# An encoder trunk of saved products: a pair of eight forms that takes 7 or 8 products by block, 12 pages instead of 13, a smaller DMA scratch and new orders

## The chip, the cores and the metric

One core of one Trainium2 chip runs the whole kernel. The metric is the device time of one execution in microseconds (us), the median of three runs. TensorE is called PE here, with its weight loads apart as PEld; VectorE is DVE, ScalarE ACT, GpSimd POOL and SyncE SP.

## What is computed

Two layers of an encoder over 256 tokens and 4096 features, in float32. Each layer normalises its input, multiplies it with one input projection of 11264 columns, runs 16 attention heads (4 of them keys and values) and 8 bidirectional retention heads on the result, gates both and multiplies their 4096 columns with an output projection, which is added to the input. A last normalisation follows.

```python
for l in range(DEPTH):                       # 2
    proj = rmsnorm(x, norm_w[l]) @ w_in[l]   # 256 x 4096 by 4096 x 11264
    aq, ak, av, ag, rq, rk, rv, rg = jnp.split(proj, SPLIT_POINTS, axis=-1)
    a_out = silu(ag) * gqa_attention(rope(rms(aq)), rope(rms(ak)), av)
    r_out = silu(rg) * rmsnorm(bidirectional_retention(rope(rq), rope(rk), rv))
    x = x + jnp.concatenate([a_out, r_out], -1) @ w_out[l]   # 256 x 4096 by 4096 x 4096
return rmsnorm(x, final_norm)
```

Nearly all of the arithmetic is in the two projections.

## The kernel before

**Blocks and pairs.** The projections are cut into 30 blocks that PE works through one after the other. A block is 256 tokens by 1024 columns (two tiles of 512, for instance keys and values). Layer 0 has input blocks 0 to 10 and output blocks 11 to 14, layer 1 has 15 to 25 and 26 to 29; these four runs are the stages 0 to 3 of the code, and `(2, 7)` in a table is the block b = 7 of stage 2, which is block 22 here. A block sums over 4096 features, cut into 16 pairs of 2 x 128 features (`NP`). For each pair the operand and the weights are 2 x 2 tiles, and the block's results collect in the eight PSUM banks M1 to M8.

**Products.** A pair takes eight products of a 128 x 128 operand tile and a 128 x 512 weight tile, or seven, by a scheme of the Strassen kind, from sums of operand tiles and sums of weight tiles. A product is three matmuls, since each float32 factor is split into a high and a low part: high by high, low by high (both at line 1760), high by low (line 1770). The six pairs 2, 5, 8, 9, 11 and 13 (`SEVENS`) take seven in every block. Pairs 3 and 6 (`FLEX`) take eight, except in the last stage: there pair 3 takes seven in blocks 27 to 29 and pair 6 in blocks 27 and 28. That makes 185 pair-blocks of seven.

**Weights.** A pair of eight has two weight pages (A and B) of 128 x 1024 in each block. SP loads each (`wraw`), ACT casts it to its high part `whi`, DVE subtracts that to get the low part `wlo`. A pair of seven has A, a sum T, a sum U and a half page B: ACT copies A to `wv`, POOL adds the weights of `twice_in` or `twice_out` to it with an accumulating DMA (line 762), DVE makes `wu` from A, `wv` and a half page `third`, and all four are cast and subtracted like the others. Five high pages (`RING`) and four low ones (`LOWS`) can stand ahead of PE.

**Operands.** At the turn from stage to stage `split_pair` (line 822) makes the operand's parts: `x8h` and `x8l`, four tiles each, for pairs of eight, `x7h` and `x7l`, seven forms each, for pairs of seven, by way of a page `xf`. For the pairs in `FLEX` a task `more_forms` (line 894) fetches the stage's input again (`again`) and makes the four further forms in two pages, `xf` and `xs`.

**Pages and tasks.** Everything else in SBUF comes from 13 pages of 4 KB a partition (`PAGES`, `page`). Attention, retention, turns and block results are tasks that run beside the products; a task starts when as many pages are free as it needs (`NEED`, and `need=` where it is added), and blocks always keep two for their own results. `attention_values` (line 1352) splits the fetched page `pT` into two new pages. Each wait that PE would have is estimated while the program is built: `Clock` and `Now` keep planned times of the engines, and constants such as `STRICT`, `LOW_AHEAD` or `RELIEF`, set for each block from `PLANS` by `assume`, say how far ahead work is put. The emitted order on each engine is fixed by this.

**Order within a block.** The first block of a stage takes its pairs in `opening_order`, with the sevens at the places given by `SPREAD` to `SPREAD3`. The others take them in the plain order of their numbers, stage 3's later blocks by `LATE_SPREAD` and `END_SPREAD`.

Of the kernel before, what the change touches and what calls it, by code (L numbers as in the profile page):

```python
# [12 lines left out]
F32R = mybir.dt.float32r  # L13
# [4 lines left out]
P = 128  # L18
# [11 lines left out]
KG = 4  # L30
# [5 lines left out]
PAGES = 13  # L36
# [46 lines left out]
NEED = {"ak": 5, "ag": 3, "rk": 4, "rg": 4}  # L83
# [28 lines left out]
    1: {'LOW_AHEAD': 5.0},  # L112
    6: {'TIGHT_A': 8},
    7: {'SUM_SLACK': 0.0, 'AT_ONCE': 1, 'STRICT': 4},
    8: {'TIGHT_B': 5, 'STRICT': 5},
    9: {'THIRD_SLACK': 1.0, 'BANK_REST': 1.5, 'LOW_AHEAD': 1.0, 'RAW_SLACK': 1.0, 'RELIEF': 0.7, 'PASS': 0.1},
    14: {'STRICT': 9, 'TIGHT_A': 0},
    15: {'S_FIXED': 0.16, 'LONG': 2, 'EARLY': 1.8, 'PASS': 0.3, 'PE_REST': 2.0, 'NEAR': 30},
    22: {'PASS': 0.3, 'U_SLACK': 1.0, 'AT_ONCE': 1},
    24: {'V_FIXED': 0.12, 'TIGHT_B': 20, 'TIGHT_A': 2},  # L120
# [9 lines left out]
SEVENS = ((2, 5, 8, 9, 11, 13), (2, 5, 8, 9, 11, 13), (2, 5, 8, 9, 11, 13), (2, 5, 8, 9, 11, 13))  # L130

FLEX = (3, 6,)

LATER = [tuple(sorted(_s + (FLEX if _i == 3 else ()))) for _i, _s in enumerate(SEVENS)]

EVER = sorted(set(_p for _s in SEVENS for _p in _s))
TWICE = sorted(EVER + list(FLEX))
EIGHTS = [_p for _p in range(NP) if _p not in EVER]
# [16 lines left out]
BLOCKS = [(("ak", 0), ("av", 0))]  # L155
BLOCKS += [(("ag", _g), ("aq", _g)) for _g in range(4)]
for _r in range(2):
    BLOCKS += [(("rk", _r), ("rq", _r))]
    BLOCKS += [(("rg", 2 * _r + _i), ("rv", 2 * _r + _i)) for _i in range(2)]
# [8 lines left out]
def constants():  # L168
# [50 lines left out]
GROUPS = [  # L219
    ([tuple(range(_s[0]))] if _s[0] else []) + [tuple(range(_a, _b)) for _a, _b in zip(_s, _s[1:] + (NP,))] for _s in LATER  # L220
]
SPREAD = (3, 5, 8, 11, 12, 13)
SPREAD1 = (4, 7, 8, 10, 12, 14)
SPREAD2 = (2, 3, 6, 7, 10, 13)
SPREAD3 = (6, 7, 9, 11, 12, 14)


def opening_order(stage):

    spread = (SPREAD, SPREAD1, SPREAD2, SPREAD3)[stage]  # L230
    spread = spread if len(spread) == len(SEVENS[stage]) else SEVENS[stage]
    order = [_p for _p in ([1, 0] if stage == 0 else [0, 1]) + list(range(2, NP)) if _p not in SEVENS[stage]]
    for i, p in zip(spread, SEVENS[stage]):
        order.insert(i, p)
    return order
# [12 lines left out]
END_FLEX = (3,)  # L248
END_SPREAD = (1, 3, 5, 7, 9, 11, 12)
LATE_SPREAD = (1, 3, 5, 6, 8, 9, 11, 12)  # L250


def late_order(sevens, spread):

    order = [_p for _p in range(NP) if _p not in sevens]
    for i, p in zip(spread or sevens, sevens):
        order.insert(i, p)
    return order


GROUPS[3] = grouped(late_order(LATER[3], LATE_SPREAD), LATER[3])
END_SEVENS = tuple(sorted(SEVENS[3] + END_FLEX))
END_GROUPS = grouped(late_order(END_SEVENS, END_SPREAD or LATE_SPREAD), END_SEVENS)


def plan_of(stage, b):

    if not b:
        return FIRST_GROUPS[stage], SEVENS[stage]
    if stage == 3 and b == N_OUT2 - 1:  # L270
        return END_GROUPS, END_SEVENS
    return GROUPS[stage], LATER[stage]
# [3 lines left out]
FIRST_GROUPS = [grouped(_o, SEVENS[_i]) for _i, _o in enumerate(FIRST_ORDER)]  # L276
LEADS = [8 * next(_i for _i, _p in enumerate(_o) if _p in SEVENS[_s]) for _s, _o in enumerate(FIRST_ORDER)]
# [91 lines left out]
def hybrid_encoder(  # L369
# [38 lines left out]
    def f32(v):  # L408
        return v.bitcast(F32)
# [412 lines left out]
    def split_pair(p, v, whole, stage):  # L822
# [15 lines left out]
        if p in SEVENS[stage]:  # L838
# [12 lines left out]
            ve.tensor_sub(s1, a22, x1[:, 0])  # L851
            ve.scalar_tensor_tensor(s2, s1, -1.0, x0[:, 0], op0=ALU.mult, op1=ALU.subtract)
            ve.tensor_sub(s3, x0[:, 0], x1[:, 0])
            ve.tensor_add(s4, x0[:, 1], s2)
            yield
            ac.copy(hi[:, 2:7, :], f)
            ve.tensor_sub(tokens(lo[:, 0:2, :]), x0, tokens(f32(hi)[:, 0:2, :]))
            yield
            ve.tensor_sub(lo[:, 2:7, :], f, f32(hi)[:, 2:7, :])
            sums_of.pop()  # L860
            drop()
        else:
            if p in EIGHTS:
                hi = t(ap, [P, 2, SEQ], "x8h", len(EIGHTS), F32R)
                lo = t(ap, [P, 2, SEQ], "x8l", len(EIGHTS), F32R)
            else:
                both = [t(ap, [P, 7, P], v, len(EVER), F32R) for v in ("x7h", "x7l")]
                hi, lo = (v[:, 0:4, :].rearrange("p (i m) t -> p i (m t)", m=MT) for v in both)
            if whole is None:
                u = [w.rearrange("p i (m a t) -> p i m a t", m=MT, t=BLK) for w in (hi, lo)]  # L870
                pieces = [(u[0][:, i], u[1][:, i], v[:, :, i]) for i in range(2)]
            else:
                pieces = [(hi, lo, whole)]
            for h, _, src in pieces:
                ac.copy(h, src)
            yield
            for h, w, src in pieces:
                ve.tensor_sub(w, src, f32(h))
        version[p] += 1
        if version[p ^ 1] == version[p]:  # L880
            drop()
        if stage == 3 and p in FLEX:
            tasks.append(Lane(more_forms(p), need=3, gate=forms_due))
# [468 lines left out]
    def attention_values(g, h, kv, sgT):  # L1352
# [4 lines left out]
        parts = parts_of("pT", [P, KG * SEQ])  # L1357
        yield from split(parts, pT)
        drop()
# [149 lines left out]
    def retention_pair(L, i, gacc, vacc):  # L1509
# [4 lines left out]
        v = yield from values(vacc, L)  # L1514
        yield
# [90 lines left out]
    def lead(stage):  # L1606

        return 8 * (late_order(LATER[3], LATE_SPREAD).index(LATER[3][0]) if stage == 3 else SEVENS[stage][0])

    def block(after_pair, phase, then, first_order=False, opening=False, order=LAST_ORDER, last=None, hurried=False):  # L1610
# [9 lines left out]
        groups, sevens = plan_of(stage, 0 if opening else N_OUT2 - 1 if last else 1)  # L1620
# [6 lines left out]
        if 0 not in SEVENS[stage] or first_order:  # L1627
# [27 lines left out]
        def begin_product(n, name, p, index, k, h):  # L1655
# [27 lines left out]
            elif p in sevens and p in FLEX:  # L1683
# [15 lines left out]
        after = 0 if not then else lead(then - 1) if then == phase else LEADS[then - 1]  # L1699

        def end_product(n, name, p, index, k, h):
# [360 lines left out]
    for l, L in enumerate(layers):  # L2062
        for bi, (one, _) in enumerate(BLOCKS):
# [10 lines left out]
            c = block(after, 2 * l + 1, 2 * l + 1 + (bi == N_IN - 1), start, bi == 0)  # L2074
# [11 lines left out]
        for n in range(N_OUT2):  # L2086
# [12 lines left out]
            if last_layer and final:  # L2099
# [4 lines left out]
                block(after, 2 * l + 2, 0, order=FINAL_ORDER, last=last_combine(res))  # L2104
                follow(True)
            else:
                if final:
                    turning.append(Turn(2 * l + 2))
                c = block(after, 2 * l + 2, 2 * l + 2 + (n == N_OUT2 - 1), opening=n == 0, hurried=n == 0)
                tasks.append(Lane(out_tasks(l, n, c), need=4, own=2))  # L2110
# [62 lines left out]
```

## Time and profile before

| | us |
|---|---|
| median of three runs | 2594.49 |
| lowest, highest | 2593.19, 2596.14 |
| the profiled execution's span | 2591.4 |
| PE busy in it | 2577.2 |
| DVE busy | 2233.3 |
| ACT busy | 1864.9 |
| POOL busy | 403.7 |

The span is from the first to the last instruction of one execution. What lies around it in a run's time, 3.1 us against the median, has no instructions. Busy times are sums over the engine's own instructions; matmuls overlap in them, so that a matmul is listed with 389 ns although the next one starts earlier.

### The profile page before, as it was taken

What the parts mean: (1) busy time and instruction counts of PE and PEld (TensorE: products, weight loads), DVE (VectorE), ACT (ScalarE), POOL (GpSimd) and SP (SyncE); (2) the same over time, 40 slices, a digit from 0 to 9 for tenths busy, and PEclk for the clock granted to TensorE, in tenths of its full rate; (3) what the DMA queues carried; (4) which work ended last, traced back from release to release, by engine and by line L of the source; (5) the groups of instructions that cost most, each with busy time, mean ns of one, the idle gap of its engine ahead of it and who ended that gap; (6) DMA issues with size and microseconds to landing.
All of it is one profiled execution on the core that took longest, in us unless ns stands there. A gap on an engine that the chain in (4) does not pass through costs nothing.

```text
span 2591.4 us, 34411 instructions
## 1 busy us (share of the span) xinstructions
PE 2577.2 (99%) x11545; PEld 2132.6 (82%) x11545; DVE 2233.3 (86%) x2740; ACT 1864.9 (72%) x2643; POOL 403.7 (16%) x555
## 2 busy tenths in 40 slices
PE   9999999999999999999999999999999999999998
PEld 7888888888888888888878888888888888888886
DVE  7898888889789898877988888889888798989887
ACT  8877776766576788655987667777666667887665
POOL 0112221221102101211111112221201021011100
PEclk9999999999999999999999999999999999999999
DMA  9988988888778777988888889888887797789986
GB/s 317 301 243 275 285 243 254 282 251 256 224 227 255 233 228 224 276 267 245 284 251 260 251 242 280 243 270 262 260 261 223 207 270 234 221 245 259 256 263 196
DMA packets 207601, 655.88 MB, mean 253 GB/s; under 512 B 24896, under 2 KB 31552, under 8 KB 207424
## 3 DMA queue, kind: packets, MB, share of 16 engines
q1 hardware_dynamic: 147040, 471.68, 51.9%
q0 software_dynamic: 59664, 180.91, 31.5%
q8 instruction: 90, 1.47, 0.2%
q10 hardware_dynamic: 720, 1.10, 0.1%
q14 instruction: 87, 0.71, 0.1%
HBM read 609.55 MB, written 44.04 MB: 252 GB/s over the span
## 4 chain that ended last, share of the span: by engine, by line
PE 97%; DVE 1%; DMA 1%; ACT 1%; issue 0%; SPq 0%; POOLq 0%; POOL 0%; DVEq 0%; ACTq 0%
PE M L1760 62%; PE M L1770 31%; PE M L1225 1%; PE M L1224 1%; PE M L1223 1%; DMA ca<-in_x 0%; PE M L1754 0%; DVE cb L353 0%; DVE wlo L353 0%; ACT ca L353 0%; DVE ca L353 0%; DMA whole<-in_w_in 0%; ACT whi L353 0%; ACT wv L353 0%; DVE x7h L353 0%
## 5 line engine op out<-in xcount | busy, mean ns | idle before, releaser
L353 DVE TENSOR_TENSOR wlo<-wraw,whi 128x1024 fp32r<-128x1024 f32 (+1 forms) x769 | 929.8, 1215 | 159.3 <-PE M L1770 52.8
L353 ACT CAST whi<-wraw 128x1024 fp32r<-128x1024 f32 (+1 forms) x771 | 795.8, 1045 | 279.1 <-PE M L1760 263.2
L1760 PE MATMUL M<-whi,x8h 128*128 128x512 f32 x2338 | 910.8, 390 | 0.5 <-DVE ca L353 0.3
L1760 PE MATMUL M<-whi,x8l 128*128 128x512 f32 x2338 | 910.0, 389 | 0.0
L1770 PE MATMUL M<-wlo,x8h 128*128 128x512 f32 x2334 | 669.4, 389 | 0.0
L1760 PEld LDWEIGHTS M<-whi,x8h 128*128 128x128 f32 x2338 | 439.0, 188 | 93.1 <-DVE ca L353 1.0
L1760 PEld LDWEIGHTS M<-whi,x8l 128*128 128x128 f32 x2338 | 439.0, 188 | 91.0 <-issue 0.2
L1770 PEld LDWEIGHTS M<-wlo,x8h 128*128 128x128 f32 x2334 | 436.5, 188 | 89.9 <-DVE wlo L353 0.7
L1760 PE MATMUL M<-whi,x7h 128*128 128x512 f32 x1080 | 420.5, 389 | 0.2 <-ACT whi L353 0.2
L1760 PE MATMUL M<-whi,x7l 128*128 128x512 f32 x1080 | 420.3, 389 | 0.0
L1770 PE MATMUL M<-wlo,x7h 128*128 128x512 f32 x1080 | 334.2, 389 | 0.2
L762 POOL DMA_DIRECT2D wv<-in_twice_in x132 | 118.5, 897 | 1068.4 <-ACT wv L353 909.3
L353 ACT CAST whi<-wu 128x1024 fp32r<-128x1024 f32 x185 | 194.6, 1052 | 98.2 <-DVE wu L353 61.5
L353 ACT CAST whi<-wv 128x1024 fp32r<-128x1024 f32 x185 | 194.2, 1050 | 87.5 <-PE M L1760 50.7
L353 DVE TENSOR_TENSOR wlo<-wv,whi 128x1024 fp32r<-128x1024 f32 x185 | 225.7, 1220 | 34.1 <-PE M L1770 26.9
L353 ACT COPY wv<-wraw 128x1024 f32<-128x1024 f32 x185 | 194.2, 1050 | 74.5 <-DMA wraw<-in_w_out 32.2
L353 DVE TENSOR_TENSOR wlo<-wu,whi 128x1024 fp32r<-128x1024 f32 x185 | 225.3, 1218 | 20.6 <-PE M L1770 13.7
L1770 PEld LDWEIGHTS M<-wlo,x7h 128*128 128x128 f32 x1080 | 202.6, 188 | 42.9 <-DVE wlo L353 1.0
L1760 PEld LDWEIGHTS M<-whi,x7h 128*128 128x128 f32 x1080 | 202.8, 188 | 42.4 <-ACT whi L353 0.8
L1760 PEld LDWEIGHTS M<-whi,x7l 128*128 128x128 f32 x1080 | 202.8, 188 | 41.7
L353 DVE TENSOR_TENSOR wu<-wraw,wv 128x512 f32<-128x512 f32 x185 | 126.6, 685 | 10.6 <-DMA wv<-in_twice_in 8.4
L353 DVE TENSOR_TENSOR wu<-wu,third 128x512 f32<-128x512 f32 x185 | 128.0, 692 | 6.4
(261 smaller groups left out, 2346.3 us busy)
## 6 DMA issues: line engine op xcount, KB each, us to landing
wraw<-in_w_in SPq DMA_DIRECT2D x568, 512.0 KB, 5.2
wraw<-in_w_out SPq DMA_DIRECT2D x203, 512.0 KB, 5.4
wv<-in_twice_in POOLq DMA_DIRECT2D x132, 512.0 KB, 7.7
third<-in_w_in SPq DMA_DIRECT2D x132, 256.0 KB, 5.7
wv<-in_twice_out POOLq DMA_DIRECT2D x53, 512.0 KB, 8.1
third<-in_w_out SPq DMA_DIRECT2D x53, 256.0 KB, 5.8
full<-next_dram POOLq DMA_DIRECT2D x18, 512.0 KB, 9.3
p_dram<-room POOLq DMA_DIRECT2D x64, 128.0 KB, 3.5
```

What stands on the lines that cost most here:

```text
L353: return call(out, *args, **kwargs)
L762: self.adds.pop(0)[1]()
L1223: nc.tensor.matmul(out, a[0], b[0], start=start, stop=False)
L1224: nc.tensor.matmul(out, a[0], b[1], start=False, stop=False)
L1225: nc.tensor.matmul(out, a[1], b[0], start=False, stop=stop)
L1760: nc.tensor.matmul(acc[name], a[i], g.hi[h], start=m == first[name] and not i, stop=False)
L1770: nc.tensor.matmul(acc[name], a, g.lo[h], start=False, stop=m == final[name])
```

## The change

Pair 6 leaves `FLEX` and the pairs of eight and becomes a pair of a new kind (`RESIDENT`): its operand holds eight forms, the four plain tiles and the four sums, made once at each of the four turns, in new tiles `xfh` and `xfl`. So each block can take seven or eight products of it; the table `ACTIVE` gives it seven in the blocks (0, 7), (2, 2), (2, 7), (3, 1) and (3, 2), which are blocks 7, 17, 22, 27 and 28. Pair 3 stays as it was, in a table by block.

Space for it: `PAGES` goes from 13 to 12, the scratch of the software DMAs from 4096 to 1024 bytes, and pair 6 gives its two tiles of eight back. `attention_values` writes the low part of `pT` into the page of `pT` itself. The pages that tasks must find free to start fall by one for the key block, for `attention_rest` and for the output blocks, and two tasks lower their claim to 3 once they have split their values.

Orders: the openings of stages 1, 2 and 3 get new places for the sevens (stage 0 keeps its own), the later blocks of stage 1 and blocks of seven sevens get new ones (`LATES`); the later blocks with six sevens in stages 0 and 2 keep the plain order. Which product leads the next block is now read from the block itself. `PLANS` is rewritten for 19 of the 30 blocks.

```diff
-PAGES = 13
+PAGES = 12
-NEED = {"ak": 5, "ag": 3, "rk": 4, "rg": 4}
+NEED = {"ak": 4, "ag": 3, "rk": 4, "rg": 4}
...
-FLEX = (3, 6,)
+RESIDENT = (6,)
+ACTIVE = {
+    6: ((0, 7), (2, 2), (2, 7), (3, 1), (3, 2)),
+}
+FLEX = {
+    (3, 1): (3,),
+    (3, 2): (3,),
+    (3, 3): (3,),
+}
...
-SPREAD = (3, 5, 8, 11, 12, 13)
-SPREAD1 = (4, 7, 8, 10, 12, 14)
-SPREAD2 = (2, 3, 6, 7, 10, 13)
-SPREAD3 = (6, 7, 9, 11, 12, 14)
+SPREADS = {
+    (0, 6): (3, 5, 8, 11, 12, 13),
+    (1, 6): (7, 9, 10, 11, 12, 14),
+    (2, 6): (1, 3, 6, 8, 13, 14),
+    (3, 6): (3, 7, 9, 10, 12, 14),
+}
...
-END_SPREAD = (1, 3, 5, 7, 9, 11, 12)
-LATE_SPREAD = (1, 3, 5, 6, 8, 9, 11, 12)
+LATES = {
+    (0, 6): (2, 5, 8, 9, 11, 13),
+    (0, 7): (2, 4, 8, 9, 11, 12, 15),
+    (1, 6): (1, 2, 5, 11, 12, 13),
...
+    (2, 7): (2, 4, 6, 8, 9, 11, 13),
+    (3, 7): (1, 2, 5, 7, 8, 11, 12),
+    (3, 8): (1, 3, 5, 6, 8, 9, 12, 14),
+}
...
-                both = [t(ap, [P, 7, P], v, len(EVER), F32R) for v in ("x7h", "x7l")]
+                both = [t(ap, [P, 8, P], v, len(RESIDENT), F32R) for v in ("xfh", "xfl")]
...
+            if p in RESIDENT:
+                yield
+                while sums_of or held[0] + pledged() >= PAGES:
+                    short[0] = not sums_of
+                    yield
...
+                f = page([P, 4, P], "xf")
+                s4, s1, s2, s3 = (tokens(f)[:, i] for i in range(4))
+                ve.tensor_sub(s1, x1[:, 1], x1[:, 0])
+                ve.scalar_tensor_tensor(s2, s1, -1.0, x0[:, 0], op0=ALU.mult, op1=ALU.subtract)
+                ve.tensor_sub(s3, x0[:, 0], x1[:, 0])
+                ve.tensor_add(s4, x0[:, 1], s2)
+                yield
+                ac.copy(both[0][:, 4:8, :], f)
+                yield
+                ve.tensor_sub(both[1][:, 4:8, :], f, f32(both[0])[:, 4:8, :])
+                sums_of.pop()
+                drop()
...
-        parts = parts_of("pT", [P, KG * SEQ])
+        parts = page([P, KG * SEQ], "pTh", F32R), pT.bitcast(F32R)
         yield from split(parts, pT)
-        drop()
...
-                tasks.append(Lane(attention_rest(L, one[1]), need=5, gate=lambda g=one[1], L=L: g in L.scored and now.t > L.scored[g] + STORE and near(LATE)))
+                tasks.append(Lane(attention_rest(L, one[1]), need=4, gate=lambda g=one[1], L=L: g in L.scored and now.t > L.scored[g] + STORE and near(LATE)))
...
-                tasks.append(Lane(out_tasks(l, n, c), need=4, own=2))
+                tasks.append(Lane(out_tasks(l, n, c), need=3, own=2))
...
-    nc = bacc.Bacc("TRN2", target_bir_lowering=False, num_devices=1, dynamic_dma_scratch_size=4096)
+    nc = bacc.Bacc("TRN2", target_bir_lowering=False, num_devices=1, dynamic_dma_scratch_size=1024)
```

## Rows read from the trace of the kernel before

**Rows 1.** The page's head: span, busy time, share and instructions of each engine.

```profile
span 2591.4 us, 34411 instructions
PE 2577.2 (99%) x11545; PEld 2132.6 (82%) x11545; DVE 2233.3 (86%) x2740; ACT 1864.9 (72%) x2643; POOL 403.7 (16%) x555
```

**Rows 2.** The page's chain of work that ended last, by engine.

```profile
PE 97%; DVE 1%; DMA 1%; ACT 1%; issue 0%; SPq 0%; POOLq 0%; POOL 0%; DVEq 0%; ACTq 0%
```

**Rows 3.** Windows: start, blocks 7, 10, 11, 13, 15, 16, 17, 26, end; PE PEld DVE ACT POOL.

```profile
0.00:5.80 5.80, 4.13 (x21) 2.81 (x21) 0.19 (x2) 2.40 (x4) 0.20 (x4) 1.00 0.65 196
...
611.90:700.80 88.90, 88.90 (x410) 74.17 (x409) 71.82 (x82) 59.51 (x75) 7.44 (x8) 1.00 0.73 216
...
872.60:959.90 87.30, 87.30 (x403) 72.96 (x402) 79.41 (x113) 70.92 (x112) 9.25 (x11) 1.00 0.79 247
959.90:1045.80 85.90, 85.90 (x392) 71.57 (x390) 76.64 (x103) 73.98 (x117) 7.59 (x9) 1.00 0.75 218
...
1128.80:1211.70 82.90, 82.90 (x367) 68.66 (x366) 64.08 (x67) 50.83 (x60) 14.42 (x20) 1.00 0.85 260
...
1294.90:1380.00 85.10, 84.51 (x367) 68.17 (x366) 70.89 (x89) 70.31 (x114) 9.67 (x12) 1.00 0.82 243
1380.00:1463.50 83.50, 83.27 (x368) 68.64 (x366) 72.98 (x95) 54.22 (x74) 14.65 (x18) 1.00 0.93 267
1463.50:1547.90 84.40, 84.40 (x379) 70.14 (x378) 71.36 (x83) 59.90 (x88) 13.10 (x17) 1.00 0.82 242
...
2248.30:2334.30 86.00, 86.00 (x391) 71.53 (x391) 79.11 (x109) 71.81 (x112) 11.02 (x12) 1.00 0.82 235
...
2579.60:2591.40 11.80, 0.38 (x2) 0.00 (x0) 4.01 (x10) 2.67 (x5) 0.56 (x1) 0.73 0.70 262
```

**Rows 4.** Groups by form: passes over a weight page; busy us, mean ns | idle before.

```profile
L353 DVE TENSOR_TENSOR wlo<-wraw,whi 128x1024 fp32r<-128x1024 f32 x763 | 925.7, 1220 | 159.1 <-PE M L1770 52.8 <-issue 50.4 <-ACT whi L353 40.9
L353 ACT CAST whi<-wraw 128x1024 fp32r<-128x1024 f32 x763 | 790.8, 1049 | 277.4 <-PE M L1760 261.5 <-ACT whi L353 5.8 <-issue 5.2
L353 DVE TENSOR_TENSOR wu<-wraw,wv 128x512 f32<-128x512 f32 x185 | 126.6, 685 | 10.6 <-DMA wv<-in_twice_in 8.4 <-DMA wv<-in_twice_out 2.2
L353 ACT CAST bhi<-third 128x512 fp32r<-128x512 f32 x185 | 114.2, 617 | 12.9 <-PE M L1760 12.7
```

**Rows 5.** Tiles xf and xs: ns min/median/max, first and last start.

```profile
L353 DVE TENSOR_TENSOR xf<-full x21: 283/284/288, 12.5 to 2274.8; 128x128 f32<-128x128 f32 x21
...
L353 ACT CAST xs<-xf x2: 622/623/624, 2295.4 to 2339.9; 128x512 fp32r<-128x512 f32 x2
L353 DVE TENSOR_TENSOR xs<-xf,xs x2: 683/684/685, 2296.4 to 2340.9; 128x512 fp32r<-128x512 f32 x2
```

**Rows 6.** Timeline of PE where blocks 15 and 16 lose time: start us, us.

```profile
1298.05 0.50 PE L1760 MATMUL M<-whi,x8h 128*128 128x512 f32 x1 [0.26 <-DVE ca L353]
...
1330.28 0.47 PE L1760 MATMUL M<-whi,x7h 128*128 128x512 f32 x1
...
1332.43 0.50 PE L1760 MATMUL M<-whi,x7h 128*128 128x512 f32 x1 [0.18 <-ACT whi L353]
...
1334.26 0.40 PE L1760 MATMUL M<-whi,x8h 128*128 128x512 f32 x1
...
1380.86 0.50 PE L1760 MATMUL M<-whi,x8h 128*128 128x512 f32 x1 [0.23 <-DVE cb L353]
```

**Rows 7.** Timelines of DVE and ACT ahead of 1330: start us, us.

```profile
1324.43 0.69 DVE L353 TENSOR_TENSOR wu<-wraw,wv 128x512 f32<-128x512 f32 x1 [2.18 <-DMA wv<-in_twice_in]
...
1321.72 4.14 ACT L353 COPY ca<-room 32x256 f32<-32x256 f32 x10
```

**Rows 8.** Timeline of POOL at the start of block 16.

```profile
1385.43 1.49 POOL L1540 DMA_DIRECT2D kv_dram<-vl  x2 [1.48 <-DVE vl L353]
1391.49 0.93 POOL L762 DMA_DIRECT2D wv<-in_twice_in  x1 [4.57 <-ACT wv L353]
```

**Rows 9.** DMA issues: count, KB each, median us from issue to landing.

```profile
kv_dram<-vl POOLq DMA_DIRECT2D x4, 256.0 KB, 8.7
```

More of the change, by code (lines that the diff above doesn't have):

```diff
@@ L127, in assume @@
     globals().update(PLANS.get(n, {}))
-SEVENS = ((2, 5, 8, 9, 11, 13), (2, 5, 8, 9, 11, 13), (2, 5, 8, 9, 11, 13), (2, 5, 8, 9, 11, 13))
-FLEX = (3, 6,)
[L134 to L138, printed above, removed]
+SEVENS = (2, 5, 8, 9, 11, 13)
+RESIDENT = (6,)
[7 more added lines that the diff above has]
+}
+FLEXED = [sorted(set(_p for (_i, _b), _v in FLEX.items() if _i == _s for _p in _v)) for _s in range(4)]
+LAST_FLEX = {(_s, _p): max(_b for (_i, _b), _v in FLEX.items() if _i == _s and _p in _v) for _s in range(4) for _p in FLEXED[_s]}
+EVER = list(SEVENS)
+TWICE = sorted(set(EVER).union(RESIDENT, *FLEXED))
+EIGHTS = [_p for _p in range(NP) if _p not in EVER and _p not in RESIDENT]
 DELAYED = tuple(EIGHTS[-4:])
@@ L154 @@
 FIRST = {"aq": AQ, "ak": AK, "av": AV, "ag": AG, "rq": RQ, "rk": RK, "rv": RVO, "rg": RG}
[L155 to L159, printed above, removed]
+FLOW = "A g0 g1 g2 g3 k0 r0 r1 k1 r2 r3"
+PARTS = {"A": ("ak", "av"), "g": ("ag", "aq"), "k": ("rk", "rq"), "r": ("rg", "rv")}
+BLOCKS = [tuple((_k, int(_b[1:] or 0)) for _k in PARTS[_b[0]]) for _b in FLOW.split()]
 N_IN = len(BLOCKS)
@@ L217, with sevens_of @@
 ]
-GROUPS = [
-    ([tuple(range(_s[0]))] if _s[0] else []) + [tuple(range(_a, _b)) for _a, _b in zip(_s, _s[1:] + (NP,))] for _s in LATER
-]
-SPREAD = (3, 5, 8, 11, 12, 13)
-SPREAD1 = (4, 7, 8, 10, 12, 14)
-SPREAD2 = (2, 3, 6, 7, 10, 13)
-SPREAD3 = (6, 7, 9, 11, 12, 14)
+SPREADS = {
[4 rows of a table added]
+}
+def sevens_of(stage, b):
+    return tuple(sorted(SEVENS + FLEX.get((stage, b), ()) + tuple(_p for _p in RESIDENT if (stage, b) in ACTIVE[_p])))
 def opening_order(stage):
[L230 to L233, printed above, removed]
+    sevens = sevens_of(stage, 0)
+    spread = SPREADS[stage, len(sevens)]
+    order = [_p for _p in ([1, 0] if stage == 0 else [0, 1]) + list(range(2, NP)) if _p not in sevens]
+    for i, p in zip(spread, sevens):
         order.insert(i, p)
@@ L245, in grouped, with order_of, lead @@
     return groups
-END_FLEX = (3,)
-END_SPREAD = (1, 3, 5, 7, 9, 11, 12)
-LATE_SPREAD = (1, 3, 5, 6, 8, 9, 11, 12)
+LATES = {
[8 rows of a table added]
+}
 def late_order(sevens, spread):
     order = [_p for _p in range(NP) if _p not in sevens]
-    for i, p in zip(spread or sevens, sevens):
+    assert len(spread) == len(sevens)
+    for i, p in zip(spread, sevens):
         order.insert(i, p)
     return order
-GROUPS[3] = grouped(late_order(LATER[3], LATE_SPREAD), LATER[3])
-END_SEVENS = tuple(sorted(SEVENS[3] + END_FLEX))
-END_GROUPS = grouped(late_order(END_SEVENS, END_SPREAD or LATE_SPREAD), END_SEVENS)
-def plan_of(stage, b):
[L268 to L272, printed above, removed]
+def order_of(stage, b):
+    if not b:
+        return FIRST_ORDER[stage]
+    sevens = sevens_of(stage, b)
+    return late_order(sevens, LATES.get((stage, len(sevens), b), LATES[stage, len(sevens)]))
+def plan_of(stage, b):
+    sevens = sevens_of(stage, b)
+    return grouped(order_of(stage, b), sevens), sevens
+def lead(stage, b):
+    sevens = sevens_of(stage, b)
+    return 8 * next(i for i, p in enumerate(order_of(stage, b)) if p in sevens)
 FIRST_ORDER = [opening_order(_i) for _i in range(4)]
-FIRST_GROUPS = [grouped(_o, SEVENS[_i]) for _i, _o in enumerate(FIRST_ORDER)]
-LEADS = [8 * next(_i for _i, _p in enumerate(_o) if _p in SEVENS[_s]) for _s, _o in enumerate(FIRST_ORDER)]
 SHARED = ("M1", "M5", "M7", "M6")
@@ L837, in split_pair @@
         x0, x1 = v[:, 0], v[:, 1]
-        if p in SEVENS[stage]:
+        if p in SEVENS:
             while sums_of or held[0] + pledged() >= PAGES:
@@ L881, in split_pair @@
             drop()
-        if stage == 3 and p in FLEX:
+        if p in FLEXED[stage]:
             tasks.append(Lane(more_forms(p), need=3, gate=forms_due))
@@ L1514, in retention_pair @@
         v = yield from values(vacc, L)
+        pledge(3)
         yield
@@ L1604, in follow, with block @@
                 finished.pop(0)[1]()
-    def lead(stage):
-        return 8 * (late_order(LATER[3], LATE_SPREAD).index(LATER[3][0]) if stage == 3 else SEVENS[stage][0])
-    def block(after_pair, phase, then, first_order=False, opening=False, order=LAST_ORDER, last=None, hurried=False):
+    def block(after_pair, phase, then, nb, first_order=False, order=LAST_ORDER, last=None, hurried=False):
         flat = []
@@ L1619, in block @@
         rush[0] = RUSH if hurried else 0.0
-        groups, sevens = plan_of(stage, 0 if opening else N_OUT2 - 1 if last else 1)
+        groups, sevens = plan_of(stage, nb)
         for g in groups:
@@ L1625, in block @@
         last_block[0] = bool(last)
-        if 0 not in SEVENS[stage] or first_order:
+        if 0 not in sevens or first_order:
             p = NATIVE[0] if first_order else 0
@@ L1682, in begin_product @@
                 a = as_it_comes[p][0][:, index[0], index[1] * P : (index[1] + 1) * P]
-            elif p in sevens and p in FLEX:
+            elif p in sevens and p in FLEXED[stage]:
                 while p not in forms:
@@ L1691, in begin_product @@
                     a = [forms[p][0][:, i, (S4, S1, S2, S3).index(index[1])] for i in range(2)]
+            elif p in RESIDENT:
+                i = (0, 2, 4, 3, 5, 6, 7)[index[1]] if p in sevens else 2 * index[0] + index[1]
+                a = at(operand[p], ALL, i)
             elif p in sevens:
@@ L1698, in block @@
         opens, shuts = final[SHARED[0]], max(first[b] for b in SHARED)
-        after = 0 if not then else lead(then - 1) if then == phase else LEADS[then - 1]
+        after = 0 if not then else lead(stage, nb + 1) if then == phase else lead(then - 1, 0)
         def end_product(n, name, p, index, k, h):
@@ L1734, in end_product @@
                 done.append(p)
+                if LAST_FLEX.get((stage, p)) == nb and not last:
+                    del forms[p]
+                    drop()
             while done and all(not left[q] for q in range(min(done))):
@@ L2073, in hybrid_encoder @@
                 turning.append(Turn(2 * l + 1))
-            c = block(after, 2 * l + 1, 2 * l + 1 + (bi == N_IN - 1), start, bi == 0)
+            c = block(after, 2 * l + 1, 2 * l + 1 + (bi == N_IN - 1), bi, start)
             ready = (lambda i=one[1], L=L: i in L.weights) if one[0] == "rg" else None
@@ L2103, in hybrid_encoder @@
                     nc.sync.dma_start(fn[i], final_norm[columns(N_OUT - 2 + i)].partition_broadcast(P))
-                block(after, 2 * l + 2, 0, order=FINAL_ORDER, last=last_combine(res))
+                block(after, 2 * l + 2, 0, n, order=FINAL_ORDER, last=last_combine(res))
                 follow(True)
@@ L2108, in hybrid_encoder @@
                     turning.append(Turn(2 * l + 2))
-                c = block(after, 2 * l + 2, 2 * l + 2 + (n == N_OUT2 - 1), opening=n == 0, hurried=n == 0)
-                tasks.append(Lane(out_tasks(l, n, c), need=4, own=2))
+                c = block(after, 2 * l + 2, 2 * l + 2 + (n == N_OUT2 - 1), n, hurried=n == 0)
+                tasks.append(Lane(out_tasks(l, n, c), need=3, own=2))
                 tasks[-1].ready = max([0.0] + landing)
```

54 lines of the change are left out of this document (34 added, 20 removed), and 2 rows, old and new, of the table LATES.

## The prediction

> **What bounds the kernel now.** I read the page's share of busy time and its chain of work first, then the windows by block, then PE's own timeline where a block is longer than its products explain. The page has PE busy for 2577.2 of 2591.4 us with 11545 matmuls [rows 1], and the chain that ended last lies on PE for 97% [rows 2]. A busy PE is not yet a bound, because matmul ends are modelled; so I take the rate from a block. Block 13 has 16 pairs, six of them with seven products: (6 x 7 + 10 x 8) x 3 = 366 matmuls of 512 columns in 82.90 us (the row counts one that reaches over its edge), 0.2267 us from start to start at a granted clock of 1.00 [rows 3]. That is the price of a matmul in this kernel, and nearly everything goes at it. What isn't at that rate is little: 5.80 us before the first product, 11.80 us after the last one [rows 3], and waits in the middle. Those the windows show when blocks with the same products are compared: block 15, which opens the second layer, takes 85.10 us for the matmuls that block 13 does in 82.90, so 2.2 us are lost in it; block 16 takes 83.50 with one record more (0.23), so 0.4 us are lost there [rows 3]. The other blocks that I compared in this way lose 0.3 us at most. So a gain can come from fewer matmuls and from about 2.9 us of waits in the middle, and hardly from elsewhere; DVE at 86% and ACT at 72% [rows 1] matter only where they let PE wait.
>
> **The products that go.** Pair 6 had eight products everywhere except in blocks 27 and 28, where it had seven. It now has seven in blocks 7, 17, 22, 27 and 28; pair 3 keeps its seven in 27 to 29 and the six others keep theirs. So 185 sevens become 188: three products or nine matmuls fewer. 9 x 0.2267 = 2.04 us. Nothing else runs beside PE's chain that could hide this, because PE is the chain; it is the firm term.
>
> **What the three new sevens cost beside it.** A pair of eight has two weight pages: 2 casts of 1.049 us on ACT and 2 subtractions of 1.220 on DVE, 2.10 and 2.44 us. A pair of seven has three full pages, a copy, two half-size adds and a half page: on ACT four passes of about 1.05 (cast A, copy, cast T, cast U) and one of 0.617, 4.82 us; on DVE 3 x 1.220 and three of about 0.685, 5.72 us [rows 4]. So DVE gets 3.3 us and ACT 2.7 us more in each of blocks 7, 17 and 22, and POOL one more accumulating DMA. Block 7 has DVE busy 71.82 of 88.90 us and block 17 71.36 of 84.40 (block 22 repeats block 7); with 3.3 more and 0.68 less PE time they stand at 85% and 89%. Block 10 has 79.41 of 87.30, 91%, and shows no lost time [rows 3]. So these three are covered on average; a local collision may cost 0 to 0.5 us each, the upper end being the wait of block 16.
>
> **The operand of eight forms.** Pair 6 gets four further forms at each of the four turns: four adds of 0.284 and one subtraction of 0.684 on DVE, 1.8 us, and one cast of 0.623 on ACT [rows 5]. Up to now that work was done once, for blocks 27 and 28, from a page fetched again by POOL; that fetch goes. Net on DVE 3 x 1.8 = 5.5 us in the whole run. The openings of the stages are where it falls. Block 11 goes from 76.64 of 85.90 us to 91% on DVE, block 15 from 70.89 of 85.10 to 85%. Block 26 has 79.11 of 86.00, 92%, and 94% with it, denser than anything that the trace has [rows 3]; one of the two sets of forms that were made from fetched pages lay in it (at 2296.4, the other at 2340.9 in block 27 [rows 5]), and if that was pair 6's its sum stays. Bounds: 0 to 1.8 us in each of blocks 11, 15 and 26. For all new waits together I take 0.5, the size of the one in block 16: of these blocks only 26 can come out denser than blocks that lose 0.3 or nothing.
>
> **The new orders.** PE's timeline says what the waits of block 15 are. At 1298.05 PE waits for DVE's last addition of the stage before [rows 6]. From 1330.28 to 1334.26 it starts twelve matmuls, 2.72 us worth, in 3.98 us, with ACT's weight cast as a releaser: 1.26 us lost [rows 6]. On DVE a weight sum waited 2.18 us at 1324.43 for the accumulating DMA, and ACT was in ten operand copies from 1321.72 for 4.14 us, so that its casts came late [rows 7]. By products the place is the pair of sevens 8 and 9, which stand next to each other in that opening. The change puts pair 6 with its eight products between them, which gives the two engines eight products of 0.68 us with only two pages to make. I count this wait as gone: -1.26. The wait at 1298 I leave: pair 2 with its costlier pages moves up to the second place there, which speaks against a gain. Block 16's wait at 1380.86, for DVE's addition into cb [rows 6], is the block's own and has the order that it had: left too. The other openings lose nothing now, so a new order can only cost there: inside the 0.5.
>
> **Pages.** A page less, but the attention that set the peak also needs one less, because the low part of pT is written over pT: 6 + 5 + 2 (scores, values, the block's own results) were 13, 6 + 4 + 2 are 12. The subtraction has the same size. I cost this at nothing; the cover is the idle time of the task queue, and if it is gone a result is combined later and PE waits for a bank, as at 1380.86.
>
> **The DMA scratch.** It shrinks from 4096 to 1024 bytes. The trace of before shows no POOL issue that is held up by it: the four stores at the start of block 16 take some 0.75 us each to issue, the second pair ending at 1386.92, and the next sum's DMA leaves at 1391.49 when ACT has its copy ready [rows 8]. So its price has no row; below it is bounded at nothing (the free issue) and above at the landing of those stores, 8.7 us [rows 9]. I take nothing, the nearer row being the issue itself, and keep the upper end as a rival. [...]
>
> **Sum.** -2.04 - 1.26 + 0.5 = -2.8 us of the profiled execution's 2591.4, so 2588.6. The runs' median is 2594.49, 3.1 us above the span; that lies around the program and I leave it: 2594.49 - 2.8 = 2591.7 us.
>
> **Rivals.** (a) All waits in the middle go: 2594.49 - 2.04 - 2.9 = 2589.6, and as much as 0.5 less with what the first block loses. For it: the waits are few and have names; against it: the two that wait for additions of the block before aren't touched by an order. (b) New waits eat the saving: the openings of blocks 11 and 26 become like that of block 15 (2.2 us each) and the three blocks with a new seven like block 16 (0.4 to 0.5 each), 2592.4 + 4.4 + 1.4 = 2598.2, and 2595 to 2596 if half of it comes. For it: 94% on DVE in block 26; against it: block 10. That a product is not saved at all belongs here (no term of -2.04). (c) Slower: POOL is held when it issues behind many-row transfers, until an earlier one has landed. The sum's DMA behind it leaves late: 1386.92 + 8.7 = 1395.6 in place of 1391.49, 4.1 us [rows 8, 9]. Queued behind it on POOL are the other stores and the small power operations; DVE's weight sum waits in order for it, and all low parts behind that sum. A sum that waited 2.18 us went with 1.26 us lost on PE [rows 6, 7], so 4.1 us late costs about 2.4. There are twelve such places (in each layer two kv stores and four fetches of rkq): 2591.7 + 29 = 2621 us. It decides from four places on, 4 x 2.4 = 9.6 us, 2601.
>
> **How the numbers follow.** The forecast, 2590 to 2594.5, has a chance of 0.65; (a) 0.14; (b) 0.11, of which 0.02 lies beyond; (c) 0.10, of which 0.08 lies beyond four places. 0.2% is 5.2 us, about what a measurement of this kernel can tell from no change: 2589.3 and 2599.7. (a) lies at the lower of these, and the three runs of before differ by 3 us; I put 0.08 of its 0.14 below it, and 0.02 of the forecast. So faster 0.10, same 0.80, slower 0.10. The range takes (a) and the half of (b) in, down to 2588.8 and up to 2597.0; what is left out is (c), the worst of (b) and the end of (a).
>
> **What would show it.** 11536 matmuls on the page. Blocks 7, 17 and 22 shorter by 0.68 us each. No wait for wlo or whi around the eighth and ninth pair of block 15, whose length comes down to about 84. The accumulating DMAs on POOL still take 0.9 us each, and the stores beside them 0.6 to 0.8; if (c) holds, some of them take several us and DVE's waits for wv grow. DVE's sum is larger by 15 us. The prediction is wrong if PE's starts are no longer 0.2267 us apart in quiet blocks, or if one opening shows more than 2 us of new waits.

## The result, and the profile after

The changed kernel takes 2606.06 us (2604.83 to 2608.86) where the kernel before, on the same chip, takes 2594.07: a ratio of 1.0046 (1.0032 to 1.0061), 12.0 us slower. The forecast was 2591.7.

The head of the page of the changed kernel:

```profile
span 2604.8 us, 34461 instructions
PE 2580.7 (99%) x11536; PEld 2133.4 (82%) x11536; DVE 2242.7 (86%) x2767; ACT 1874.0 (72%) x2657; POOL 407.6 (16%) x557
```

Nine matmuls are gone, and the span is 13.4 us longer than that of [rows 1]. The windows by block, as in [rows 3], say where: blocks 2, 7, 15, 16 and 17 of the changed kernel (us, then busy time of PE, PEld, DVE, ACT and POOL, granted clock, DMA share, GB/s).

```profile
177.20:263.40 86.20, 85.26 (x379) 69.91 (x378) 76.86 (x98) 60.30 (x91) 17.20 (x24) 1.00 0.89 267
...
615.70:702.40 86.70, 86.70 (x395) 72.17 (x394) 73.27 (x83) 59.40 (x70) 7.41 (x9) 1.00 0.80 223
...
1298.20:1387.40 89.20, 85.18 (x368) 69.78 (x368) 72.14 (x97) 72.92 (x119) 9.56 (x11) 0.98 0.78 231
1387.40:1477.40 90.00, 85.94 (x367) 70.58 (x366) 72.51 (x93) 54.65 (x74) 14.69 (x18) 0.96 0.83 243
1477.40:1561.20 83.80, 83.80 (x376) 69.59 (x376) 74.27 (x87) 62.44 (x91) 14.11 (x18) 1.00 0.83 247
```

Block 16 takes 90.00 us where it took 83.50, block 15 89.20 for 85.10. Their granted clock is below 1.00, which it was nowhere in the middle before. What PE waits for in block 16 can be followed backwards through three timelines of the changed kernel (start us, us; in brackets the idle time before, and what ended it): POOL, DVE, PE.

```profile
1389.82 0.80 POOL L1598 DMA_DIRECT2D kv_dram<-vh  x1 [4.89 <-ACT vh L392]
1396.10 0.78 POOL L1598 DMA_DIRECT2D kv_dram<-vh  x1 [5.49 <-ACT whi L392]
1409.39 0.75 POOL L1598 DMA_DIRECT2D kv_dram<-vl  x1 [12.50 <-DVE ca L392]
1412.42 0.76 POOL L1598 DMA_DIRECT2D kv_dram<-vl  x1 [2.29 <-issue]
1413.17 0.95 POOL L801 DMA_DIRECT2D wv<-in_twice_in  x1
```

```profile
1418.70 0.69 DVE L392 TENSOR_TENSOR wu<-wraw,wv 128x512 f32<-128x512 f32 x1 [7.46 <-DMA wv<-in_twice_in]
```

```profile
1421.31 2.07 PE L1830 MATMUL M<-wlo,xfh 128*128 128x512 f32 x4 [4.06 <-DVE wlo L392]
1423.18 0.63 PE L1820 MATMUL M<-whi,x7h 128*128 128x512 f32 x1
1423.61 0.63 PE L1820 MATMUL M<-whi,x7l 128*128 128x512 f32 x1
```

The four stores of the values, 0.75 us each before [rows 8], now go out over 23 us. The weight sum's DMA behind them, the last line of POOL, waits with them; DVE stands 7.46 us for its landing, all low parts stand behind that sum, and PE stands 4.06 us. The brackets of the second and third store name ACT and DVE, but what these two stores need was ready long before: the high parts were made by 1389.93, the low parts by 1391.98. What comes 0.30 to 0.36 us before each of the last three stores is the landing of the store ahead of it, at 1395.74, 1409.09 and 1412.12. What follows PE's wait is new too: PE's next starts are 0.43 us apart, not 0.2267, for 6 us.

In block 15 it is the addition of the last residual. `cb<-in_x` followed `ca<-in_x` by 0.7 us before; now:

```profile
1301.12 1.23 POOL L1936 DMA_DIRECT2D ca<-in_x  x1 [0.32 <-issue]
1313.12 1.22 POOL L1936 DMA_DIRECT2D cb<-in_x  x1 [10.76 <-issue]
```

```profile
1364.79 0.51 PE L1820 MATMUL M<-whi,x8h 128*128 128x512 f32 x1 [3.82 <-ACT x8h L392]
1365.49 0.65 PE L1820 MATMUL M<-whi,x8l 128*128 128x512 f32 x1 [0.20 <-DVE x8l L392]
```

The last tile of the stage comes from that addition, so pair 14's operand is late by the time PE asks for it. For other held issues the profile names nothing that it knows ("issue"). The largest two such groups of POOL (us in total, times, longest); in the trace of before no group of that kind is over 1 us in total:

```profile
POOL rkq L1489 <- issue: 57.3, 10, 8.0
...
POOL cb L1936 <- issue: 18.3, 2, 10.8
```

### The profile page after: what moved, and what is told of

It is laid out like the page before. It is cut to its first block, busy times and chain, and to the rows that moved or that the text cites. A ratio compares the mean times of both kernels' runs of the same rounds, so it can differ in the third digit from the quotient of the medians.

```text
span 2604.8 us, 34461 instructions
## 1 busy us (share of the span) xinstructions
PE 2580.7 (99%) x11536; PEld 2133.4 (82%) x11536; DVE 2242.7 (86%) x2767; ACT 1874.0 (72%) x2657; POOL 407.6 (16%) x557
## 4 chain that ended last, share of the span: by engine, by line
PE 90%; issue 3%; DMA 2%; DVE 2%; ACT 2%; POOL 0%; DVEq 0%; SPq 0%; ACTq 0%; POOLq 0%
PE M L1820 58%; PE M L1830 29%; DMA wv<-in_twice_in 1%; PE M L1280 1%; PE M L1282 1%; PE M L1281 1%; DVE wlo L392 1%; DMA full<-in_xT 1%; ACT whi L392 1%; DMA x_dram<-ca 0%; DMA wraw<-in_w_in 0%; ACT ca L392 0%; DVE ca L392 0%; DVE cb L392 0%; ACT cb L392 0%
## 5 line engine op out<-in xcount | busy, mean ns | idle before, releaser
L392 DVE TENSOR_TENSOR wlo<-wraw,whi 128x1024 fp32r<-128x1024 f32 x766 | 925.7, 1215 | 163.7 <-PE M L1830 65.2
L1820 PE MATMUL M<-whi,x8h 128*128 128x512 f32 x2110 | 822.5, 390 | 3.8 <-ACT x8h L392 3.8
L1820 PE MATMUL M<-whi,x8l 128*128 128x512 f32 x2110 | 822.2, 390 | 0.2 <-DVE x8l L392 0.2
L1830 PE MATMUL M<-wlo,x8h 128*128 128x512 f32 x2106 | 608.2, 390 | 0.7 <-DVE wlo L392 0.5
L1820 PEld LDWEIGHTS M<-whi,x8h 128*128 128x128 f32 x2110 | 396.5, 188 | 86.5 <-ACT x8h L392 4.2
L1820 PEld LDWEIGHTS M<-whi,x8l 128*128 128x128 f32 x2110 | 396.6, 188 | 83.0 <-DVE x8l L392 0.5
L1830 PEld LDWEIGHTS M<-wlo,x8h 128*128 128x128 f32 x2106 | 394.2, 188 | 83.1 <-DVE wlo L392 2.4
```

What stands on the lines that cost most here:

```text
L392: return call(out, *args, **kwargs)
L1820: nc.tensor.matmul(acc[name], a[i], g.hi[h], start=m == first[name] and not i, stop=False)
L1830: nc.tensor.matmul(acc[name], a, g.lo[h], start=False, stop=m == final[name])
```

## The experiments

Two theories stood at the start. R: the cut scratch holds POOL. O: the new orders, the eight forms or the missing page make the waits. The first three runs change one number.

**The changed kernel with 4096 and with 2048 bytes, the kernel before with 1024.**

```diff
-dynamic_dma_scratch_size=1024
+dynamic_dma_scratch_size=4096
```

> The changed kernel with the scratch of the software DMAs back at 4096 bytes, nothing else touched. Theory R (POOL is held when the descriptors of transfers under way fill the scratch): the kv stores go out 0.8 us apart again, cb<-in_x goes out right behind ca<-in_x (10.8 us later now), PE's waits of 4.0 us at 1364.8 and 4.2 us at 1421.3 and the half clock behind them go, and the time is 2590 to 2594 us, the forecast of 2591.7 among it. Theory O (the new orders, the eight forms or the twelfth page make the waits, the scratch does nothing): the waits stay where they are and the time stays at 2603 to 2608 us.

Measured: 2595.14 us (2593.55 to 2596.82) beside 2593.70 of before, ratio 1.0005 (0.9997 to 1.0014). 10.9 us less than the changed kernel, and 1.4 above the kernel before, a difference that the interval doesn't tell from none. The two residual additions go out one behind the other again:

```profile
1299.98 1.22 POOL L1936 DMA_DIRECT2D ca<-in_x  x1 [0.16 <-issue]
1300.70 1.74 POOL L1936 DMA_DIRECT2D cb<-in_x  x1
```

Block 16 takes 82.90 us, block 2 84.50. But the time is not the forecast's 2591.7: 3.4 us are left, and block 15 still takes 86.90 us. O is wrong as the main cause and not quite wrong as a small one.

> The kernel before with only the scratch cut from 4096 to 1024 bytes. R: POOL issues of many-row transfers (kv stores, rkq fetches, cb<-in_x) are held by 3 to 11 us each, sums come late behind them, and the time rises to 2599 to 2612 us. O: 2593 to 2596 us, no POOL issue later than before.

Measured: 2611.83 us, ratio 1.0068 (1.0055 to 1.0080): 18.1 us slower, by the scratch alone; it does more harm to the kernel before than to the changed one. The hold is at the same instruction:

```profile
1308.78 1.23 POOL L1876 DMA_DIRECT2D ca<-in_x  x1 [2.77 <-DVE xf L353]
1320.69 1.22 POOL L1876 DMA_DIRECT2D cb<-in_x  x1 [10.67 <-issue]
```

> The changed kernel with 2048 bytes, half way. [...] If each byte of scratch matters evenly, it would lie half way, 2597 to 2600. O: 2603 to 2608.

Measured: 2595.80 us (2594.92 to 2597.27), 1.0007 (0.9998 to 1.0016), the same as with 4096, and below both ranges. So the price is not even by the byte: half the scratch costs no time that these runs can tell, a quarter costs 10.9 us. One long hold is left with 2048 bytes, the fourth store of the values in block 16:

```profile
1389.03 0.74 POOL L1598 DMA_DIRECT2D kv_dram<-vl  x1 [0.48 <-DVE vl L392]
1395.10 0.76 POOL L1598 DMA_DIRECT2D kv_dram<-vl  x1 [5.33 <-DVE blo L392]
```

PE doesn't wait behind it: it is busy through all of that block, 83.00 us.

**Rows under way, or bytes?** With 1024 bytes kept, the values' stores were given wider rows (`...` leaves out the new DRAM tile and the fetches that read it).

```diff
-                nc.gpsimd.dma_start(
-                    kv_dram[:, :, 2 + i, k * HD : (k + 1) * HD].rearrange("g p d -> p g d"),
-                    v[i][:, k, :].rearrange("p (g d) -> p g d", g=4),
-                )
+                nc.gpsimd.dma_start(v_dram[:, i, k, :], v[i][:, k, :])
...
```

> The changed kernel with its 1024 bytes, but the four stores of the values go out as 128 rows of 2 KB and not as 512 of 512 bytes, into a DRAM tile of their own; the same bytes. The eight fetches of values become two DMAs of 256 rows of 512 bytes each. Theory D (POOL is held by the number of rows under way, for which the scratch has room): the four stores go out 0.8 us apart, the wait near 1421 and its half clock (7.2 us together) go, and the time falls from 2606 to 2597 to 2601 us; the hold of cb<-in_x and the wait behind it (6.3 us) stay. Rival B (bytes or transfers under way are what counts): the stores are held as before and the time stays at 2604 to 2608.

Measured: 2600.05 us (2598.41 to 2603.02), 6.0 us less than the changed kernel. The same 256 KB each, in a quarter of the rows, go out at once:

```profile
1390.84 1.17 POOL L1602 DMA_DIRECT2D v_dram<-vh  x2 [4.80 <-ACT vh L392]
1392.78 0.53 POOL L1602 DMA_DIRECT2D v_dram<-vl  x1 [0.77 <-DVE vl L392]
1393.49 0.53 POOL L1602 DMA_DIRECT2D v_dram<-vl  x1 [0.18 <-issue]
```

Block 16's wait is gone and block 15's stays (3.4 us at 1365.22), as D said. The fourth store leaves at 1393.49, before the first one lands at 1396.05, so four transfers with 1 MB are under way together in the same 1024 bytes; the changed kernel too has up to seven transfers, and up to 2.5 MB, under way elsewhere. So neither the bytes nor the number of transfers is what was full: by these runs it is the rows. What a row takes of the scratch they don't show.

**What is left with 4096 bytes: is it pair 14's place?** In the new opening of block 15 pair 14 stands fourth from the end; before it was the last but one. Block 15 of the kernel with 4096 bytes, and PE's wait in it:

```profile
1297.40:1384.30 86.90, 85.12 (x368) 69.79 (x367) 72.19 (x96) 72.78 (x119) 9.56 (x11) 0.98 0.81 239
```

```profile
1361.66 0.49 PE L1820 MATMUL M<-whi,x8h 128*128 128x512 f32 x1 [1.56 <-ACT x8h L392]
1362.37 0.75 PE L1820 MATMUL M<-whi,x8l 128*128 128x512 f32 x1 [0.22 <-DVE x8l L392]
```

The kernel with 4096 bytes was changed in one entry:

```diff
-    (2, 6): (1, 3, 6, 8, 13, 14),
+    (2, 6): (1, 3, 6, 8, 11, 13),
```

> The changed kernel with 4096 bytes of scratch and one entry of its orders changed: in block 15's opening the sevens stand at (1, 3, 6, 8, 11, 13) in place of (1, 3, 6, 8, 13, 14), so pair 14 is again the last but one of the sixteen and not the fourth from the end. Theory S: the wait at 1361.7 of the kernel with 4096 bytes (1.7 us for x8h, 0.5 for x8l, some 2 us of half clock behind them) is the price of asking for pair 14 two pairs, some 9.5 us, earlier; it goes, and the time falls by 3.5 to 4.5 us, to about 2591. Theory T (the operand is late whatever the order, for want of ACT's time): a wait of 1 us or more stays at pair 14 or 15, and the time falls by less than 2 us.

Measured: 2594.89 us, 1.0004 (0.9995 to 1.0013): no gain. S fell in this form. The wait moved with the pair (PE, then ACT):

```profile
1367.50 0.50 PE L1820 MATMUL M<-whi,x8h 128*128 128x512 f32 x1 [0.74 <-ACT x8h L392]
1369.33 0.65 PE L1820 MATMUL M<-whi,x8l 128*128 128x512 f32 x1 [1.32 <-DVE x8l L392]
```

```profile
1359.29 1.65 ACT L392 COPY cb<-room 32x256 f32<-32x256 f32 x4
1360.96 2.00 ACT L392 CAST whi<-wraw 128x1024 fp32r<-128x1024 f32 x2
...
1365.95 0.90 ACT L392 ACTIVATE cb<-cb,nw 128x256 f32<-128x256 f32 x2
```

The page of pairs 14 and 15 is ready at 1360.9, and its scaling starts 5 us later, behind five weight passes. In the code an operand that comes late is put to be split only when the pair at work is finished or its own is asked for. So this rule was changed, once alone and once together with the place (`...` leaves out the two lines that set `here` to the stage at work).

```diff
             late.append((c, stage))
+            if here[0] == stage and stage == 2:
+                split_late()
...
```

> The changed kernel with 4096 bytes, with one change of when work is put: in the opening of stage 2 an operand that comes late (pairs 12 and 13, 14 and 15) is put to be split as soon as its page is ready, and not at the end of the next pair. If the wait of 1.7 us for pair 14 comes from the time between its page and its split, it shrinks; with pair 14 in its new early place the page itself is ready only just before, so I expect 0 to 1.5 us less than the 2595.1 of the kernel with 4096 bytes.

Measured: 2593.22 us, 0.9998 (0.9989 to 1.0007), 1.9 us less than without by the medians, somewhat more than expected; the two intervals overlap. A wait of 1.1 us stays at 1359.7.

> The same with pair 14 late as well. In the run with pair 14 late alone the last copies of the page ended at 1360.9 as before the change, but its scaling began only at 1365.95, behind weight casts, and PE waited at 1367.5. Put at once, it should be scaled by about 1362 and the wait (2.5 us and 1.9 us of half clock) should go: 2590 to 2592 us. If it stays near 2595, the wait is due to ACT's lack of time.

Measured: 2592.25 us (2591.20 to 2592.93) beside 2593.80, ratio 0.9992 (0.9983 to 1.0001). Now the scaling starts right behind the next cast, and PE doesn't wait at all in block 15, 83.00 us (ACT, then the window):

```profile
1359.57 1.65 ACT L392 COPY cb<-room 32x256 f32<-32x256 f32 x4
1361.25 1.05 ACT L392 CAST whi<-wraw 128x1024 fp32r<-128x1024 f32 x1
1362.20 0.91 ACT L392 ACTIVATE cb<-cb,nw 128x256 f32<-128x256 f32 x2
```

```profile
1297.20:1380.20 83.00, 83.00 (x368) 68.75 (x367) 72.20 (x97) 72.21 (x119) 9.58 (x11) 1.00 0.84 248
```

Neither alone is enough: the early split without the late place leaves 1.1 us, the late place without the early split all of it. This kernel has the lowest median of all that ran; it is 1.5 us below the kernel before, which its interval just doesn't tell from no change.

**The planning constants.** Once the kernel with pair 14 late and without the new entry for block 0:

```diff
-    0: {'V_FIXED': 0.085, 'LATE': 35, 'RAW_SLACK': 0, 'EARLY': 1.8, 'U_SLACK': 0.6, 'LOW_AHEAD': 5, 'SUM_SLACK': 0.3},
```

> The same with the new entry of PLANS for block 0 left out, so that block 0 is planned as in the kernel before. If that entry makes the waits for wlo at 33 to 60 us (1.2 us together), they go and this is 1 to 1.5 us below the kernel with pair 14 late alone. If the further forms of pair 6 at the first turn make them, they stay and the times are alike.

Measured: 2602.70 us, 1.0034 (1.0021 to 1.0046), 7.8 us slower than with the entry. Neither of the two answers came: the waits for wlo go, and larger ones for the operands take their place (PE in block 0).

```profile
62.92 0.50 PE L1819 MATMUL M<-whi,x8h 128*128 128x512 f32 x1 [0.85 <-ACT x8h L391]
65.88 0.57 PE L1819 MATMUL M<-whi,x8l 128*128 128x512 f32 x1 [2.45 <-DVE x8l L391]
```

Something in the changed kernel makes block 0's operands later than before, where the same constants have no such wait; the new entry takes them forward and pays some 1.2 us of waits for wlo. That this something is the further forms of pair 6, which are made in that block, is likely and was not tried apart.

Once with all nine entries of the kernel before in place of the new table (4096 bytes):

> The changed kernel with 4096 bytes and the PLANS of the kernel before, all nine entries, with the new orders. S: the wait for pair 14 near 1362 stays within 1 us of what it was (it is the order's), while the waits at 33 to 60 and at 891 (1.3 us) may go: 2592 to 2596 us. Rival P (the new planning constants make all new waits): the wait near 1362 goes too, 2589 to 2592.

Measured: 2604.71 us, 1.0041 (1.0027 to 1.0055). The wait for pair 14 is there, and larger (2.8 us at 1369.62), so P falls for it; S's number falls too, since the waits in block 0 don't go but grow as in the run above. The new constants are worth 9.6 us to the changed kernel.

**The three products alone.**

```diff
-    6: ((0, 7), (2, 2), (2, 7), (3, 1), (3, 2)),
+    6: ((3, 1), (3, 2)),
```

> The changed kernel with 4096 bytes, but pair 6 takes eight products in blocks 7, 17 and 22, as before the change. If the three saved products are worth their 2.04 us, this is 2.0 us slower than the kernel with 4096 bytes, about 2597.2; blocks 7, 17 and 22 are 0.68 us longer each. If the three sevens cost waits by their 3.3 us of DVE each, it is less than 1 us slower.

Measured: 2597.32 us, 1.0013 (1.0004 to 1.0022); 2.2 us more than with the products by the medians, where the two intervals overlap. The profiles say it more sharply: from first matmul to first matmul block 17 takes 84.44 us for 83.76, block 22 88.82 for 88.11, blocks 7 and 8 together 176.17 for 175.49.

**The order and the early split, in the kernel before.**

```diff
-SPREAD2 = (2, 3, 6, 7, 10, 13)
+SPREAD2 = (1, 3, 6, 8, 11, 13)
```

together with the early split shown above.

> The kernel before (4096 bytes, 13 pages, no pair of eight forms, its own planning constants) with two things alone: block 15's opening takes the sevens at (1, 3, 6, 8, 11, 13), so that pair 6 stands between 8 and 9, and an operand that comes late in that opening is put to be split at once. If the wait at 1330 to 1334 was due to 8 and 9 standing side by side, it goes, and perhaps those at 1298 and 1380 with it: 1.3 to 2.9 us less than before, 2591 to 2592.5. If its planning constants and page count are what made those waits, they stay: 2593.5 to 2595.

Measured: 2592.62 us beside 2593.45, 0.9997 (0.9988 to 1.0006), just outside the first of the two ranges. The waits at 1330 to 1334 and at 1380.86 are gone: block 15 takes 84.10 us for 85.10, block 16 83.00 for 83.50. The gain in block 15 would be larger but for the wait at its start for DVE's addition of the stage before, which was 0.26 us in [rows 6] and is 0.83 now. Blocks 15 and 16, then PE at the start of block 15:

```profile
1294.70:1378.80 84.10, 83.27 (x367) 68.61 (x366) 71.74 (x92) 70.54 (x114) 9.58 (x11) 1.00 0.85 248
1378.80:1461.80 83.00, 83.00 (x368) 68.72 (x367) 72.33 (x93) 55.04 (x74) 14.69 (x18) 1.00 0.91 263
```

```profile
1296.18 0.50 PE L1762 MATMUL M<-whi,x8h 128*128 128x512 f32 x1 [0.83 <-DVE cb L353]
```

So the wait between pairs 8 and 9 goes, as predicted. Two things were changed at once here, but the early split concerns pairs 12 to 15, and the wait is absent without it too, in the kernel with 4096 bytes; so it goes to the order. What both are worth in all, 0.8 us by the medians, is within what the interval leaves open.

## Why the prediction was wrong

The blocks side by side, us, from the windows of each kernel:

| block | before | changed | changed, 4096 | pair 14 late, split at once |
|---|---|---|---|---|
| 0 | 86.50 | 88.70 | 88.60 | 88.10 |
| 2 | 84.50 | 86.20 | 84.50 | 84.50 |
| 15 | 85.10 | 89.20 | 86.90 | 83.00 |
| 16 | 83.50 | 90.00 | 82.90 | 82.90 |
| 17 | 84.40 | 83.80 | 83.80 | 83.80 |

**The term that failed: the scratch.** "I take nothing, the nearer row being the issue itself". That row [rows 8] was of a kernel with four times the room, so it could not be near: it shows what an issue costs while there is room. Three runs give the term its size: 10.9 us in the changed kernel, 18.1 in the one before, and at 2048 bytes nothing that they can tell. The mechanism had been written down as rival (c), with a chance of 0.10. Its sign, issues that take several us, did not come in that form: each store still takes 0.75 us, and the hold stands as idle time ahead of it.

What was under way could have been counted in the trace of before. Counted with the one that is issued, 52 of its 521 POOL issues have 1024 rows or more under way, and the most is 2048, the four stores of 512 rows. The changed kernel never has more than 896. Two of its stores would make 1024, and in both layers each did leave only when the one ahead had landed, 0.30 to 0.37 us after it. With 2048 bytes the store that was held for 5.33 us is the fourth of 512 rows. One hold is not covered: cb<-in_x has 256 rows, with those of ca<-in_x 512, yet in all four places the changed kernel sent it 0.33 us after ca<-in_x had landed. Why it takes more room than its rows say stays open.

**Rival (c) was right in kind and wrong in price.** It said 2.4 us a place and twelve places, 29 us. The trace has 57.3 us of idle time before fetches of rkq that cost PE nothing that I found, because nothing of PE's hangs on them soon; the loss sits in a few places. In block 16 the wait and the slow clock behind it are 7 us, in block 2 1.7, and in block 15 2.3 is the difference between 89.20 and 86.90. I also missed `cb<-in_x` among the places, where POOL is held up to 10.76 us; only the third store of block 16 waits longer, 12.50.

**The products: right.** -2.04 us. Block 17 is 0.6 us shorter, blocks 7 and 8 together 175.5 for 176.2 (attention work moved from the one to the other), and without the three products the time is 2.2 us longer. That DVE's 3.3 us in each of these blocks are covered was right too: none of them shows a wait. DVE's busy time on the page grew by 9.4 us and not by 15; summed pass by pass it is 14.1 more, 2400.8 where the page has 2242.7, so overlapping passes count once on the page.

**The wait between pairs 8 and 9: right.** It is in none of the kernels that have an eight between them, the changed one among them. The two that I left in the sum, at 1298 and 1380.86, went or stayed from kernel to kernel.

**New waits, taken at 0.5 us: wrong.** In the profile with 4096 bytes they are about 7: its span is 3.4 us above that of before, where 3.3 should have gone. That execution is the slowest of its eleven; by the medians they are 4.7. Two places carry most of them, block 10 (below) some more; the openings of blocks 11 and 26, which I had looked at, are only 0.4 and 0.3 us longer. In block 15 I looked at which sevens stand side by side and not at pair 14, which the same list of places moves two pairs forward: the operand that is made last is asked for 9.5 us earlier. It costs 2.2 us of waits and 1.7 at the lower clock (0.98 over the block), together the 3.9 between 86.90 and 83.00, and is mended by the place and the early split together. In block 0 I had put nothing: I spoke of the openings of blocks 11, 15 and 26 and forgot that the first stage has a turn too, where all operands are made while PE already runs. Block 0 is 2.1 us longer. It starts 0.4 us earlier and spends that waiting for its first loads; of the 1.7 us by which it ends later, 1.2 are waits for wlo.

**Open.** In block 10 six of the seven profiles of the changed kernel's variants with 4096 bytes have a wait of 0.8 to 1.35 us near 891 to 898, and the one with the early split alone has none. In the kernel with 4096 bytes and no other change ACT waits there for weights whose load takes 9.2 us beside two fetches of rkq, 7.6 before and 7.8 in the profile without the wait; what makes the load slower was not tried. Whether the twelfth page costs anything was not tried by itself. Nor was the end of the program, 0.3 us longer in all kernels of the new kind.

## What to carry to other kernels

A number that sets the size of a shared room, as the scratch here, has no price in a trace that was taken with more of it: count what is under way at once in that trace, in the unit that fills the room, and compare it with the new size. Where PE is the bound at 99%, look for each thing that is made last in a stage and ask whether an order moves its use forward; the mean load of the engines says nothing on that. A held store can be a late load for what the same engine issues behind it: here the four stores went out over 23 us, and DVE stood 7.46 us for the weight sum's DMA behind them.

## What the runs showed of the hardware

**GpSimd's DMA issues were held in order, by rows.** With 1024 bytes of scratch they were held up to 12.5 us, and the weight sum's DMA behind a held store waited with it, until 1413.17; with 2048 bytes two stores of the values were held, 5.3 and 0.8 us, with 4096 none. With 1024 bytes, stores of 512 rows of 512 bytes were held and those of 128 rows of 2 KB with the same bytes weren't.

**A wait of PE cost more than its length.** After the wait of 4.06 us that ended at 1421.31 the granted clock was 0.51 for 6 us, and the next matmuls were 0.43 us apart. The windows of the changed kernel before, in and after that stretch:

```profile
1417.00:1421.30 4.30, 0.25 (x2) 0.00 (x0) 2.56 (x4) 2.52 (x4) 0.00 (x0) 0.88 0.43 101
1421.30:1427.30 6.00, 5.99 (x14) 4.70 (x15) 6.00 (x6) 5.77 (x6) 0.94 (x1) 0.51 0.97 236
1427.30:1431.00 3.70, 3.70 (x18) 3.02 (x17) 3.70 (x11) 1.33 (x2) 3.14 (x5) 1.00 1.03 360
```

Fourteen matmuls at 0.43 us in place of 0.2267 are 2.8 us on top of the 4.06. It doesn't follow from the length of the wait alone: behind 1.56 us at 1361.66 the kernel with 4096 bytes ran some eight matmuls at 0.43, behind 1.55 at the same place the one without the three products ran at 0.23, and so did the one with the old constants behind 2.81. What decides between the two was not tried.
